# Eight more tile pairs of a four-layer trunk as products of half-size blocks, and one product placed earlier

## The chip, the cores and the metric

The kernel runs on one core of a Trainium2 chip. The metric is the device time of one execution in microseconds (us). The core's engines work side by side, each through its own queue in order: TensorE (PE) multiplies, VectorE (DVE) and GpSimd (POOL) add and subtract, ScalarE (ACT) copies and applies functions, SyncE (SP) starts most transfers.

## The reference, cut to what matters

Four layers, each `x += mixer(rmsnorm(x))` and then a layer end:

```
x += sigmoid(x @ pg_w[i]) * (p[i] @ pe_w[i])      # pg_w[i]: 1024 x 1024, pe_w[i]: 256 x 1024
```

Here x has 520 rows (512 of a prompt, 8 of a sample group) and 1024 columns. Everything is wanted in fp32. The mixers of the four layers are a matrix memory (layer 0), a gated short convolution (layer 1), windowed attention (layer 2) and causal pooling (layer 3); the code counts layers from 0.

## The kernel before

x lies in SBUF transposed, as eight tiles of 128 x 520 floats (`self.x[j]`). A product in fp32 is made from three products of numbers with shorter mantissas: an operand is split into a high part (`hi`, `wh`, made by ACT) and the rest (`lo`, `wl`, made by DVE from the operand and the high part), and PE adds up hi·wh, lo·wh and hi·wl. An output tile of 520 columns is made in two parts (256 and 264), so that a plain tile with eight tiles of input (`proj`) costs 8 x 3 x 2 = 48 matmuls.

`seven()` makes a pair of output tiles otherwise: weights and x are seen as 2 x 2 blocks (two output tiles by two halves of the input; two halves of x's 520 columns), and seven products of half size, of 12 matmuls of 260 columns each, with sums of weight blocks and sums of x blocks, take the place of eight: 84 matmuls for 96. The products are called "11", "T2", "T1", "21", "T3", "T4" and "22". The copy `s1` of "11" (line 378, ACT) must be made before "21" may add into the same accumulator; `u2` (line 381, DVE) and `u3` (line 390) are sums on the way to the outputs. "22" of a pair is held back in `self.pend` and issued later by `flush()`: in the middle of the next plain tile, or inside the next `seven()`. Before the change only the convolution's input projection in layer 1 is made so (19 pairs; `summed()`, lines 583 to 603, makes the row sums: four POOL subtractions, ACT copies `ha`, `hb`, DVE rests `la`, `lb` for each of four k).

The layer end is `embed()`. Each tile j takes 12 matmuls of the small product (`pe`) and 48 of the gate (`pg`), 60 in all. Then, in this chain: ACT's sigmoid (line 648), two DVE multiplies (line 650), a DVE add into x (line 651), ACT's `hi` of the next layer's input (line 470), ACT's square for the next norm (line 515 or 518), DVE's `lo` (line 471). The next tile's matmuls run meanwhile. Ahead of it `out_proj()` makes the x tiles one by one (line 628) and splits them.

Weights are brought in by SP (`wf`), split or summed ahead of use by ACT, DVE and POOL; a planner (`plan()`, `due()`) orders these operations by the cost of the matmuls that come before, and `pump()` issues them in the engines' queues between the other work. For some weights (`MOVED`) ACT makes the negative of `wh` and POOL starts a transfer that adds the weights to it in place of DVE's subtraction. Streams of small steps (`tick()`) are issued along the matmuls.

Of the kernel before, what the change touches and what calls it, by code (L numbers as in the profile page):

```python
# [22 lines left out]
KD = 8  # L23
# [16 lines left out]
NPLAIN = 3  # L40
HALF = T // 2
FBUFS, HBUFS, SBUFS = 4, 4, 4
MOVED = ("w_b", "w_bo")


class Item:


    def __init__(self, *keys, cost=5.76, life=None):
        self.keys, self.cost, self.life = keys, cost, life  # L50
        name, j = keys[0][:2]
        self.moved = name in MOVED and not (name == "w_b" and j % 16 == 0)


def paired(j):
# [4 lines left out]
def plan():  # L60

    out = []
    add = lambda *key, **kw: out.append(Item(key, **kw))

    def end(i, name, halves, begun=False):
        cs = range(2 if halves else 1)
        for c in cs:
            for j in range(2):
                if c or not begun:
                    last = c == len(cs) - 1 or i == 1  # L70
                    add(name, j, *([c] if halves else []), life=(2 - j) * 5.76 if last else None)
        for j in range(2, KD):
            for c in cs:
                add(name, j, *([c] if halves else []))
        for j in range(KD):
            if j % 4 == 0:
                add("w_pe", i, j // 4, cost=0, life=28.8)
            add("w_pg", i, j, cost=7.2)

    for hd in range(H):  # L80
        for j in (hd, 8 + hd, 16 + 2 * hd, 17 + 2 * hd, 32 + 2 * hd, 33 + 2 * hd):
            add("w_a", j)
    for j in range(16):
# [110 lines left out]
class Net:  # L194
# [47 lines left out]
    def make(self, i, op):  # L242

        if (i, op) in self.made:
            return
        self.made.add((i, op))
        nc, it = self.nc, self.items[i]
        t = self.wt.setdefault(i, {})
        f = lambda tile: tile.bitcast(F32)
        new = lambda tag, n=1024, pool=None, dt=F32R: (pool or self.wp).tile([P, n], dt, tag=tag, name=self.nm(tag))  # L250

        def high(k, tag, n=1024, pool=None):
            t["h" + k] = new(tag, n, pool)
            nc.scalar.activation(t["h" + k], t["w" + k], AF.Copy)  # L254

        def low(k, tag, n=1024, pool=None):
            t["l" + k] = new(tag, n, pool)
            if k == "1" and it.moved:
                nc.scalar.activation(t["l1"], f(t["h1"]), AF.Copy, scale=-1.0)  # L259
                key = it.keys[0]  # L260
                nc.gpsimd.dma_start(t["l1"], self.d[key[0]][key[1:]], accum_op=ALU.add)  # L261
                return
            nc.vector.tensor_sub(t["l" + k], t["w" + k], f(t["h" + k]))  # L263

        a, b = slice(0, 512), slice(512, 1024)
        sub = nc.gpsimd.tensor_sub
        if op in ("load", "load2"):
            n = 2 if op == "load2" else 1
            key = it.keys[n - 1]
            t[f"w{n}"] = self.wp.tile([P, 1024], F32, tag="wf", name=self.nm("wf"), bufs=FBUFS)  # L270
            nc.sync.dma_start(t[f"w{n}"], self.d[key[0]][key[1:]])
        elif op == "split":
            high("1", "wh")
            low("1", "wl")
        elif op == "sum":
            w1, w2 = t["w1"], t["w2"]
            s1, s2, s4 = (self.act()[:, :512] for _ in range(3))
            nc.gpsimd.tensor_add(s1, w2[:, a], w2[:, b])
            sub(s2, s1, w1[:, a])
            sub(w2[:, a], w1[:, a], w2[:, a])  # L280
            sub(s4, w1[:, b], s2)
            t.update(ws1=s1, ws2=s2, ws4=s4)
        else:
            k = op.removeprefix("high").removeprefix("low") or "1"
            step = high if op.startswith("high") else low
            if k[0] == "s":
                step(k, op[0] + "s", 512, self.sp)
            else:
                step(k, "w" + op[0])
# [49 lines left out]
            mm(out[j], wl, a[0][:, PARTS[j]], start=False, stop=stop)  # L339
        self.pump(0.72)  # L340

    def seven(self, keys, B, dst, done):

# [23 lines left out]
        def step():  # L367
            self.pump(1.44)
            self.tick()
# [12 lines left out]
        step()  # L382
        product(r5, part("s1"), "T1", True)
        step()
        product(r1, part("1", b), "21", False)
        nc.scalar.activation(dst[0][:, :HALF], r1, AF.Copy)
        step()
        self.flush()
        product(r6, part("2", a), "T3", False)
        add(u3, r6, s1)  # L390
        step()
        product(r4, part("2", b), "T4", True)
        pair = lambda x, n: x.rearrange("p (u c) -> p u c", u=2)[:, :, :n]
# [220 lines left out]
    def out_proj(self, name, y, i, begun=None):  # L614

        nc = self.nc
        xs = []
        first = begun or self.proj_pair(name, y, 8 if i == 2 else 16)
        self.pt = [self.act() for _ in range(2)]
        for k in range(2):  # L620
            nc.sync.dma_start(self.pt[k], self.d["pT"][i, k])
        for j in range(KD):
            if j in (3, 4):
                self.pt[j - 3] = self.split(self.pt[j - 3])
            if j == 0:
                *_, pair = first
            ps = pair[j] if j < 2 else self.proj(name, j, a=y)
            nc.vector.tensor_add(self.x[j], ps, self.x[j])  # L628
            xs.append(self.split(self.x[j]))
        self.look = 0  # L630
        return xs

    def embed(self, i, xs):

        nc, d = self.nc, self.d
        hs, we = [], None
        g0 = C_NG + (i + 1) * KD
        for j in range(KD):
            if j % 4 == 0:
                we = self.weights("w_pe", i, j // 4)  # L640
# [3 lines left out]
            if i == 3 and j == KD - 1:  # L644
                return self.final(xs, pe, hs)
            pg = self.proj("w_pg", i, j, a=xs)
            sg = self.act()
            nc.scalar.activation(sg, pg, AF.Sigmoid)  # L648
            for u in range(2):
                nc.vector.tensor_mul(sg[:, PARTS[u]], self.part(pe, u), sg[:, PARTS[u]])  # L650
            nc.vector.tensor_add(self.x[j], self.x[j], sg)
            if i < 3:
                hs.append(self.split(self.x[j], self.col(g0 + j)))
            else:
                hs.append(self.act())
                nc.scalar.activation(hs[j], self.x[j], AF.Copy, scale=self.col(C_FG + j))
            self.square_in(j)
        self.sums = {} if i == 0 else None
        self.finish_norm(hs, g0, 3, *((4, 1), (2, 3), (0, 0))[i], sums=self.sums)
        return hs  # L660

    def final(self, xs, pe, xg):
# [8 lines left out]
        xg.append(self.act())  # L671
# [46 lines left out]
    def mlstm(self, h, lay):  # L718
# [3 lines left out]
        with ExitStack() as st:  # L722
# [330 lines left out]
    def conv(self, h, lay):  # L1053
# [4 lines left out]
        with ExitStack() as st:  # L1058
# [387 lines left out]
    def pooling(self, h, lay):  # L1446
# [3 lines left out]
        with ExitStack() as st:  # L1450
# [68 lines left out]
    def run(self):  # L1519
# [32 lines left out]
        for i, (mixer, w) in enumerate(  # L1552
            ((self.mlstm, "w_ao"), (self.conv, "w_bo"), (self.attention, "w_co"), (self.pooling, "w_do"))
        ):
            with ExitStack() as lay:
# [4 lines left out]
            h = self.embed(i, xs)  # L1560


OUTS = {
# [124 lines left out]
```

## Time and profile before

| | |
|---|---|
| median of three executions | 2163.52 us (2162.26 to 2165.96) |
| the profiled execution | 2164.99 us |
| its span | 2163.2 us |
| PE busy | 2131.4 us, 99% |
| DVE, ACT, POOL busy | 1388.3, 899.8, 406.6 us |
| TensorE's granted clock, mean | 0.999 |

The span runs from the first to the last instruction in the trace; the 1.8 us beside it belong to the execution and not to the engines' work. Busy time of PE counts a matmul from its start to a modelled end, so idle time between matmuls and the list of waits say more than the 99%.

### The profile page before, as it was taken

How to read it: one execution, taken by the hardware profiler on the slowest of the kernel's cores; microseconds unless marked ns; L12 is line 12 of the kernel's file. 1: busy time of each engine (PE TensorE's matmuls, PEld its weight loads, DVE VectorE, ACT ScalarE, POOL GpSimd, SP SyncE). 2: the span in 40 equal slices, each digit the busy share in tenths (PEclk: the TensorE clock that was granted, in tenths of full speed). 3: DMA queues.
4: the chain of work that ended last, by engine and by line, in shares of the span. 5: the costliest groups of instructions: out<-in, count | busy, mean ns of one | idle time of the engine just before them, and what ended most of it. 6: DMA issues, size and time to landing. Idle time of an engine off the chain costs nothing.

```text
span 2163.2 us, 42666 instructions
## 1 busy us (share of the span) xinstructions
PE 2131.4 (99%) x17560; PEld 2111.3 (98%) x17560; DVE 1388.3 (64%) x3064; ACT 899.8 (42%) x1434; POOL 406.6 (19%) x487
## 2 busy tenths in 40 slices
PE   8999999999999999999999999999999999999998
PEld 8999999999999999999999999999999999999998
DVE  7677667653566666651478887787876566676434
ACT  6445443432455554564333333333344342222233
POOL 1111100100035545521014332332320000000000
PEclk9999999999999999999999999999999999999999
DMA  5654454332266676678333465555555233222421
GB/s 164 195 174 140 160 179 160 99 98 92 85 147 158 158 177 154 157 191 190 91 130 118 159 200 179 180 171 177 184 162 178 95 110 98 89 97 92 126 79 50
DMA packets 112951, 305.22 MB, mean 141 GB/s; under 512 B 34260, under 2 KB 38612, under 8 KB 110708
## 3 DMA queue, kind: packets, MB, share of 16 engines
q1 hardware_dynamic: 104404, 272.54, 38.9%
q0 software_dynamic: 8208, 29.89, 8.0%
q8 instruction: 138, 2.26, 0.4%
q14 instruction: 57, 0.47, 0.1%
q10 hardware_dynamic: 144, 0.06, 0.0%
HBM read 279.63 MB, written 22.82 MB: 140 GB/s over the span
## 4 chain that ended last, share of the span: by engine, by line
PE 76%; DVE 9%; DMA 5%; issue 4%; ACT 4%; POOL 2%; SPq 0%; ACTq 0%; DVEq 0%; POOLq 0%
PE ps L335 21%; PE ps L339 20%; PE ps L337 20%; DVE wl L263 2%; ACT wh L254 1%; PE ax L337 1%; PE ax L339 1%; PE ax L335 1%; PE ax L363 1%; PE ax L365 1%; PE ax L1335 1%; PE ax L364 1%; DMA kc<-kc 1%; DVE kc L460 1%; DMA wl<-w_b 1%
## 5 line engine op out<-in xcount | busy, mean ns | idle before, releaser
L335 PE MATMUL ps<-hi,wh 128*128 128x256 f32 x4672 | 963.5, 288 | 2.5 <-DVE a L486 1.5
L339 PE MATMUL ps<-hi,wl 128*128 128x256 f32 x4672 | 940.4, 283 | 0.9 <-DMA wl<-w_bo 0.7
L337 PE MATMUL ps<-lo,wh 128*128 128x256 f32 x4672 | 938.7, 282 | 0.4 <-DVE lo L1137 0.2
L335 PEld LDWEIGHTS ps<-hi,wh 128*128 128x128 f32 x4672 | 726.0, 188 | 8.6 <-issue 1.5
L337 PEld LDWEIGHTS ps<-lo,wh 128*128 128x128 f32 x4672 | 724.8, 188 | 0.8 <-DVE lo L1137 0.4
L339 PEld LDWEIGHTS ps<-hi,wl 128*128 128x128 f32 x4672 | 723.0, 188 | 1.5 <-DMA wl<-w_bo 0.9
L263 DVE TENSOR_TENSOR wl<-wf,wh 128x1024 fp32r<-128x1024 f32 x287 | 363.4, 1270 | 159.4 <-ACT wh L254 156.8
L254 ACT ACTIVATE wh<-wf 128x1024 fp32r<-128x1024 f32 x344 | 360.9, 1053 | 158.2 <-issue 90.9
L1212 POOL TENSOR_TENSOR a<-a,a 32x520 f32<-32x520 f32 x48 | 70.3, 1465 | 282.6 <-ACT a L503 103.1
L503 ACT ACTIVATE a<-ps 128x520 f32<-128x520 f32 x42 | 47.5, 1130 | 137.4 <-PE ps L339 118.9
L628 DVE TENSOR_TENSOR x<-ps,x 128x520 f32<-128x520 f32 x32 | 22.3, 698 | 122.8 <-PE ps L339 122.7
L1213 POOL TENSOR_TENSOR a<-a,a 32x520 f32<-32x520 f32 x48 | 70.8, 1475 | 129.9 <-DVE a L1211 117.1
L490 ACT ACTIVATE a<-a 128x520 f32<-128x520 f32 x42 | 26.8, 639 | 155.2 <-DVE a L486 155.2
L467 ACT ACTIVATE hi<-x 128x520 fp32r<-128x520 f32 x32 | 20.4, 639 | 156.4 <-DVE x L628 156.4
L486 DVE TENSOR_TENSOR a<-ps,a 128x520 f32<-128x520 f32 x85 | 58.9, 692 | 21.0 <-PE ps L339 17.6
L263 DVE TENSOR_TENSOR ls<-a,hs 128x512 fp32r<-128x512 f32 x57 | 64.5, 1142 | 12.0 <-ACT hs L254 12.0
L650 DVE TENSOR_TENSOR a<-ax,a 128x256 f32<-128x256 f32 (+1 forms) x62 | 23.7, 423 | 72.6 <-ACT a L648 72.6
L1238 ACT ACTIVATE S<-S,nmx 128x128 f32<-128x128 f32 (+1 forms) x96 | 39.9, 417 | 66.7 <-DVE nmx L1235 66.5
L460 DVE CUSTOM_DVE_ANT_0 kc<-kc,qb 128x128 f32<-128x128 f32 (+1 forms) x192 | 54.4, 340 | 14.2 <-DMA kc<-kc 14.2
L460 DVE CUSTOM_DVE_ANT_0 vc<-vc,pb 128x128 f32<-128x128 f32 (+1 forms) x192 | 62.9, 384 | 0.0
L261 POOL DMA_DIRECT2D wl<-w_b x41 | 36.3, 885 | 137.8 <-ACT wl L259 122.2
L259 ACT ACTIVATE wl<-wh 128x1024 fp32r<-128x1024 f32 x57 | 60.5, 1061 | 1.8
(344 smaller groups left out, 2874.8 us busy)
## 6 DMA issues: line engine op xcount, KB each, us to landing
wf<-w_c SPq DMA_DIRECT2D x80, 512.0 KB
wf<-w_a SPq DMA_DIRECT2D x64, 512.0 KB
wf<-w_b SPq DMA_DIRECT2D x64, 512.0 KB
wl<-w_b POOLq DMA_DIRECT2D x41, 512.0 KB, 6.6
wf<-w_pg SPq DMA_DIRECT2D x32, 512.0 KB
wf<-w_d SPq DMA_DIRECT2D x32, 512.0 KB
pb<-scr_p SPq DMA_DIRECT2D x8, 1292.0 KB
Ci<-C_in SPq DMA_DIRECT2D x16, 512.0 KB
```

The costliest lines, as they stand in the source:

```text
L254: nc.scalar.activation(t["h" + k], t["w" + k], AF.Copy)
L259: nc.scalar.activation(t["l1"], f(t["h1"]), AF.Copy, scale=-1.0)
L263: nc.vector.tensor_sub(t["l" + k], t["w" + k], f(t["h" + k]))
L335: mm(out[j], wh, a[0][:, PARTS[j]], start=start, stop=False)
L337: mm(out[j], wh, a[1][:, PARTS[j]], start=False, stop=False)
L339: mm(out[j], wl, a[0][:, PARTS[j]], start=False, stop=stop)
L460: self.nc.vector.tensor_tensor_reduce(junk, a, b, 1.0, 0.0, ALU.mult, ALU.add, out)
L486: nc.vector.tensor_mul(dst[:, :T], ps, self.r)
L503: nc.scalar.activation(dst, split(ps), AF.Copy)
L1212: nc.gpsimd.tensor_mul(b[:32], t[:32], cs[0])
L1213: nc.gpsimd.tensor_mul(a[:32], a[:32], cs[1])
L1238: nc.scalar.activation(blk, blk, AF.Exp, bias=nmx[:, i : i + 1], scale=SCALE, accum_out=l[:, i : i + 1])
```

## The change

In each layer's end the gate's tiles (1, 2) and (4, 5) are made by `seven()`: 84 matmuls for a pair in place of 96. The row sums of x that this needs are made by the new `crossed()`, one step for each pair of x tiles (k, k + 4): four POOL subtractions of 128 x 260, two ACT copies and two DVE subtractions of 128 x 520. It is queued as a stream when tile k + 4 of `out_proj` is done, and what is left of it is issued (`drain`) ahead of the first pair. `beside()` gives buffers for it. Inside `seven()` the held product "22" of the pair before now comes behind "T1" rather than behind "21"; this holds for the convolution too. Tile j + 1 of a pair is ended (`early`) behind "T4", and tile j behind "22", which is issued in the middle of the next tile's gate. The weights of these pairs are summed by POOL (four operations), and the low part of a pair's first weight goes by the POOL transfer (`moved`).

```diff
+EPAIRS = (1, 4)
...
-            add("w_pg", i, j, cost=7.2)
+            if j in EPAIRS:
+                out.append(Item(("w_pg", i, j), ("w_pg", i, j + 1), cost=12.96))
+            elif j - 1 not in EPAIRS:
+                add("w_pg", i, j, cost=7.2)
...
         product(r5, part("s1"), "T1", True)
         step()
+        self.flush()
         product(r1, part("1", b), "21", False)
         nc.scalar.activation(dst[0][:, :HALF], r1, AF.Copy)
         step()
-        self.flush()
         product(r6, part("2", a), "T3", False)
         add(u3, r6, s1)
         step()
         product(r4, part("2", b), "T4", True)
         pair = lambda x, n: x.rearrange("p (u c) -> p u c", u=2)[:, :, :n]
         add(pair(dst[1], HALF), pair(v, HALF), u3.unsqueeze(1).broadcast_to([P, 2, HALF]))
+        if early:
+            early()
         step()
         self.pend = last
...
             xs.append(self.split(self.x[j]))
+            if j > 3:
+                self.side.gens.append(self.crossed(j - 4, xs))
...
+    def crossed(self, k, xs):
+
+        nc, B = self.nc, self.xsums
+        a, b = slice(0, HALF), slice(HALF, T)
+        sub = nc.gpsimd.tensor_sub
+        t, u = self.x[k], self.x[k + 4]
+        ta, tb = self.act(), self.act()
+        sub(ta[:, a], t[:, b], t[:, a])
+        sub(ta[:, b], u[:, b], ta[:, a])
+        sub(tb[:, a], u[:, b], t[:, b])
+        sub(tb[:, b], u[:, a], ta[:, b])
+        for _ in range(4):
+            yield
...
+        hs = room("ha"), room("hb")
+        for h, x in zip(hs, (ta, tb)):
+            nc.scalar.activation(h, x, AF.Copy)
+        yield
+        ls = room("la"), room("lb")
+        for h, l, x in zip(hs, ls, (ta, tb)):
+            nc.vector.tensor_sub(l, x, h.bitcast(F32))
...
+        def two(j, we):
+            sg = self.act(), self.act()
+            end = lambda n: lambda: ends(j + n, part(we, j + n), sg[n], sg[n])
+            self.seven((("w_pg", i, j), ("w_pg", i, j + 1)), self.xsums, sg, end(0), end(1))
+
+        for j in range(KD):
+            if j % 4 == 0:
+                we = self.weights("w_pe", i, j // 4)
+            if j in EPAIRS:
+                self.side.drain()
+                two(j, we)
+            elif j - 1 not in EPAIRS:
+                pe = part(we, j)
+                if i == 3 and j == KD - 1:
+                    return self.final(xs, pe, hs)
+                pg = self.proj("w_pg", i, j, a=xs)
+                ends(j, pe, self.act(), pg)
```

The order of instructions shows where this puts the work. First ACT's queue at the start of layer 0's end, before; `x_85` to `x_92` are the eight x tiles, and a name's number tells one buffer use from another:

```order
L648 ACT_TABLE_LOAD
L648 ACTIVATE a_6525<-ps_6474 128x520
L470 ACTIVATE hi_6530<-x_85,cols 128x520
L515 ACTIVATE a_6534<-x_85 128x520
L254 ACTIVATE wh_6551<-wf_6316 128x1024
L648 ACTIVATE a_6605<-ps_6550 128x520
```

The same place after (the sigmoid is line 696 now, `hi` 479, the square 524, a weight's high part 261, the row sums' copies 666, `s1` 385):

```order
L696 ACT_TABLE_LOAD
L696 ACTIVATE a_6596<-ps_6523 128x520
L479 ACTIVATE hi_6601<-x_85,cols 128x520
L524 ACTIVATE a_6605<-x_85 128x520
L666 ACTIVATE ha_6607<-a_6542 128x520
L666 ACTIVATE hb_6608<-a_6543 128x520
L261 ACTIVATE wh_6619<-wf_6350 128x1024
L385 ACTIVATE a_6626<-ax_6623 128x260
L394 ACTIVATE a_6615<-ax_6623 128x260
```

The copies `ha`, `hb` of the fourth row sum (k = 3) stand behind the whole end of tile 0, and `s1` of the first pair behind them. Then the second pair of the same layer, ACT's queue after the change; `x_86` is tile 1, `x_88` tile 3, and `hs` the high part of a weight sum:

```order
L696 ACTIVATE a_6615<-a_6615 128x520
L479 ACTIVATE hi_6830<-x_86,cols 128x520
L527 ACTIVATE a_6834<-x_86 128x520
L261 ACTIVATE hs_6837<-a_6721 128x512
L696 ACTIVATE a_6865<-ps_6764 128x520
L479 ACTIVATE hi_6870<-x_88,cols 128x520
L527 ACTIVATE a_6874<-x_88 128x520
L261 ACTIVATE wh_6877<-wf_6594 128x1024
L385 ACTIVATE a_6886<-ax_6883 128x260
```

The end of tile 1 now comes directly ahead of the end of tile 3, and the second pair's `s1` (the last row) behind both. In layer 2 two of the four row sums come late; ACT's queue there after the change:

```order
L696 ACTIVATE a_20780<-ps_20707 128x520
L479 ACTIVATE hi_20785<-x_85,cols 128x520
L524 ACTIVATE a_20789<-x_85 128x520
L666 ACTIVATE ha_20791<-a_20726 128x520
L666 ACTIVATE hb_20792<-a_20727 128x520
L666 ACTIVATE ha_20805<-a_20799 128x520
L666 ACTIVATE hb_20806<-a_20800 128x520
L261 ACTIVATE wh_20817<-wf_20520 128x1024
L385 ACTIVATE a_20824<-ax_20821 128x260
```

Four copies stand there in place of two, those of k = 2 and of k = 3. Next POOL's queue in layer 0 after the change, around the fourth row sum (lines 653 to 656); lines 285 to 288 sum the second pair's weights:

```order
L268 DMA wl_6457<-w_pg 128x1024
L653 TENSOR_TENSOR a_6542<-x_88 128x260
L654 TENSOR_TENSOR a_6542<-x_92,a_6542 128x260
L655 TENSOR_TENSOR a_6543<-x_92,x_88 128x260
L656 TENSOR_TENSOR a_6543<-x_92,a_6542 128x260
L285 TENSOR_TENSOR a_6719<-wf_6594 128x512
L286 TENSOR_TENSOR a_6720<-a_6719,wf_6562 128x512
L287 TENSOR_TENSOR wf_6594<-wf_6562,wf_6594 128x512
L288 TENSOR_TENSOR a_6721<-wf_6562,a_6720 128x512
```

The sums for the second pair follow at once, as soon as their weights have landed. Last the convolution: PE's queue in the last of three pairs in a row, before, where "T1" (`ps_8507`) ends and "21" (`ax_8505`) begins:

```order
L363 MATMUL ps_8507<-ha_7740,hs_8432 128x260
L364 MATMUL ps_8507<-la_7742,hs_8432 128x260
L365 MATMUL ps_8507<-ha_7740,ls_8461 128x260
L363 MATMUL ax_8505<-hi_7289,wh_8333 128x260
L364 MATMUL ax_8505<-lo_7305,wh_8333 128x260
L365 MATMUL ax_8505<-hi_7289,wl_8337 128x260
```

And after, at the end of the same "T1" (`ps_8605`):

```order
L370 MATMUL ps_8605<-ha_7838,hs_8539 128x260
L371 MATMUL ps_8605<-la_7840,hs_8539 128x260
L372 MATMUL ps_8605<-ha_7838,ls_8559 128x260
L370 MATMUL ps_8466<-hi_7387,hs_8458 128x260
L371 MATMUL ps_8466<-lo_7403,hs_8458 128x260
L372 MATMUL ps_8466<-hi_7387,ls_8462 128x260
```

The twelve matmuls of the pair before's "22" (`ps_8466`) now stand between "T1" and "21".

## Rows read from the trace of the kernel before

**Rows 1.** The page's head: span, and busy time of each engine.

```profile
span 2163.2 us, 42666 instructions
...
PE 2131.4 (99%) x17560; PEld 2111.3 (98%) x17560; DVE 1388.3 (64%) x3064; ACT 899.8 (42%) x1434; POOL 406.6 (19%) x487
```

**Rows 2.** Waits of PE: what waited, for what; us in total, times, longest.

```profile
PE ps L335 <- ACT a L1542: 5.2, 1, 5.2
PE ax L363 <- ACT a L378: 5.0, 6, 0.8
PE ax L1306 <- DVE S L1298: 4.2, 4, 2.0
```

**Rows 3.** Line 378 (`s1`): who waited for it, us and times.

```profile
  PEld ax L363: 6.3, 6
```

**Rows 4.** Timeline of ACT, layer 0's end: start, duration, line, idle before.

```profile
553.82 0.60 ACT L648 ACTIVATE a<-ps 128x520 f32<-128x520 f32 x1 [3.57 <-PE ps L339]
555.99 0.73 ACT L470 ACTIVATE hi<-x,cols 128x520 fp32r<-128x520 f32 x1 [1.56 <-DVE x L651]
556.63 0.62 ACT L515 ACTIVATE a<-x 128x520 f32<-128x520 f32 x1
557.16 1.04 ACT L254 ACTIVATE wh<-wf 128x1024 fp32r<-128x1024 f32 x1
561.00 0.60 ACT L648 ACTIVATE a<-ps 128x520 f32<-128x520 f32 x1 [2.80 <-PE ps L339]
```

**Rows 5.** Timeline of PE where the second tile's matmuls begin.

```profile
553.62 0.40 PE L335 MATMUL ax<-hi,wh 128*128 128x256 f32 x2
```

**Rows 6.** Timeline of ACT, layer 2's end.

```profile
1715.36 0.60 ACT L648 ACTIVATE a<-ps 128x520 f32<-128x520 f32 x1 [3.55 <-PE ps L339]
...
1718.70 1.04 ACT L254 ACTIVATE wh<-wf 128x1024 fp32r<-128x1024 f32 x1
```

**Rows 7.** Timeline of PE, the convolution's third pair: "T1", "21", "22".

```profile
719.47 0.28 PE L365 MATMUL ps<-ha,ls 128*128 128x260 f32 x1
720.59 0.39 PE L363 MATMUL ax<-hi,wh 128*128 128x260 f32 x1 [0.83 <-ACT a L378]
...
722.12 0.28 PE L363 MATMUL ps<-hi,hs 128*128 128x260 f32 x1
```

**Rows 8.** Timelines of ACT and DVE at the same place.

```profile
720.16 0.37 ACT L378 ACTIVATE a<-ax 128x260 f32<-128x260 f32 x1
...
718.67 0.70 DVE L394 TENSOR_TENSOR a<-ps,a 128x520 f32<-128x520 f32 x1
```

**Rows 9.** Timelines of ACT and DVE: a row sum's copies and rests.

```profile
659.32 0.62 ACT L600 ACTIVATE ha<-a 128x520 fp32r<-128x520 f32 x1
...
659.98 0.70 DVE L603 TENSOR_TENSOR la<-a,ha 128x520 fp32r<-128x520 f32 x1 [3.27 <-ACT ha L600]
```

**Rows 10.** Timeline of DVE in layer 0's end.

```profile
554.46 0.76 DVE L650 TENSOR_TENSOR a<-ax,a 128x256 f32<-128x256 f32 x2 [4.25 <-ACT a L648]
556.76 0.76 DVE L471 SCALAR_TENSOR_TENSOR lo<-x,cols,hi 128x520 fp32r<-128x520 f32 x1 [0.80 <-ACT hi L470]
```

**Rows 11.** Timelines of DVE and POOL in the convolution.

```profile
704.42 0.67 DVE L263 TENSOR_TENSOR ls<-a,hs 128x512 fp32r<-128x512 f32 x1
...
706.02 2.61 DVE L263 TENSOR_TENSOR ls<-a,hs 128x512 fp32r<-128x512 f32 x1
...
706.49 1.58 POOL L278 TENSOR_TENSOR a<-wf 128x512 f32<-128x512 f32 x1
```

**Rows 12.** Timeline of PE, the first matmuls of the program.

```profile
8.86 0.64 PE L335 MATMUL ps<-hi,a 128*64 128x256 f32 x2
9.29 0.64 PE L337 MATMUL ps<-lo,a 128*64 128x256 f32 x2
...
14.08 0.40 PE L335 MATMUL ps<-hi,a 128*64 128x256 f32 x2
14.32 0.40 PE L337 MATMUL ps<-lo,a 128*64 128x256 f32 x2
```

More of the change, by code (lines that the diff above doesn't have):

```diff
@@ L51, in __init__ @@
         name, j = keys[0][:2]
-        self.moved = name in MOVED and not (name == "w_b" and j % 16 == 0)
+        self.moved = name in MOVED and not (name == "w_b" and j % 16 == 0) or name == "w_pg" and len(keys) > 1
 def paired(j):
@@ L249, in make, with new @@
         f = lambda tile: tile.bitcast(F32)
-        new = lambda tag, n=1024, pool=None, dt=F32R: (pool or self.wp).tile([P, n], dt, tag=tag, name=self.nm(tag))
+        def new(tag, n=1024, pool=None):
+            if pool is self.ap:
+                return self.act(F32R, tag)[:, :n]
+            return (pool or self.wp).tile([P, n], F32R, tag=tag, name=self.nm(tag))
         def high(k, tag, n=1024, pool=None):
@@ L340, in mm6, with seven @@
         self.pump(0.72)
-    def seven(self, keys, B, dst, done):
+    def seven(self, keys, B, dst, done, early=None):
         nc = self.nc
@@ L618, in out_proj @@
         first = begun or self.proj_pair(name, y, 8 if i == 2 else 16)
+        self.side, self.xsums = Stream(1), {n: [] for n in ("11", "21", "22", "T1", "T2", "T3", "T4")}
+        self.streams = [*self.streams, self.side]
         self.pt = [self.act() for _ in range(2)]
@@ L629, in out_proj, with room, beside, part @@
             xs.append(self.split(self.x[j]))
+            if j > 3:
+                self.side.gens.append(self.crossed(j - 4, xs))
         self.look = 0
         return xs
+    def crossed(self, k, xs):
[10 more added lines that the diff above has]
+            yield
+        def room(s):
+            self.spare -= 1
+            return self.act(F32R, s, self.ep if self.spare >= 0 else None)
+        hs = room("ha"), room("hb")
[5 more added lines that the diff above has]
+            nc.vector.tensor_sub(l, x, h.bitcast(F32))
+        for n, (h, l), c in (("11", xs[k], a), ("21", xs[k + 4], a), ("22", xs[k + 4], b),
+                             ("T1", (hs[0], ls[0]), a), ("T2", (hs[0], ls[0]), b),
+                             ("T3", (hs[1], ls[1]), a), ("T4", (hs[1], ls[1]), b)):
+            B[n].append((h[:, c], l[:, c]))
+        yield
+    def beside(self, lay, n):
+        pool = lambda name, **kw: lay.enter_context(self.tc.tile_pool(name=self.nm(name), **kw))
+        self.sp = pool("ws", bufs=SBUFS)
+        self.ep, self.spare = pool("ep", bufs=n), n
     def embed(self, i, xs):
         nc, d = self.nc, self.d
-        hs, we = [], None
+        hs, we = [None] * KD, None
         g0 = C_NG + (i + 1) * KD
-        for j in range(KD):
-            if j % 4 == 0:
-                we = self.weights("w_pe", i, j // 4)
+        def part(we, j):
             pe = self.aux(), self.aux()
@@ L643, in embed, with ends @@
                 self.mm6(pe, we, ((j % 4) * 2 + k) * P, self.pt[k], k == 0, k == 1)
[L644 to L647, printed above, removed]
+            return pe
+        def ends(j, pe, sg, pg):
             nc.scalar.activation(sg, pg, AF.Sigmoid)
@@ L652, in embed @@
             if i < 3:
[L653 removed]
+                hs[j] = self.split(self.x[j], self.col(g0 + j))
             else:
[L655 removed]
+                hs[j] = self.act()
                 nc.scalar.activation(hs[j], self.x[j], AF.Copy, scale=self.col(C_FG + j))
             self.square_in(j)
+        def two(j, we):
[14 more added lines that the diff above has]
+                ends(j, pe, self.act(), pg)
         self.sums = {} if i == 0 else None
@@ L670, in final @@
         x, sg, sq = self.x[j], self.act(), self.act()
-        xg.append(self.act())
+        xg[j] = self.act()
         ch = lambda t, c: t[:, c * n : (c + 1) * n]
@@ L778, in mlstm @@
         ex = lay.enter_context(tc.tile_pool(name="mly", bufs=16))
+        self.beside(lay, 3)
         self.streams = [self.gate]
@@ L1149, in conv @@
             nc.sync.dma_start(d["o_conv_s"], so)
+        self.beside(lay, 3)
         return y
@@ L1205, in attention @@
         self.finish = finish
+        self.sp, self.ep, self.spare = self.ap, None, 0
         return y
@@ L1475, in pooling @@
             nc.sync.dma_start(d["o_pool_s"], sp[:, :, 1:16])
+        self.beside(lay, 10)
         return y, first
@@ L1559, in run @@
                 xs = self.out_proj(w, y, i, first)
-            h = self.embed(i, xs)
+                h = self.embed(i, xs)
 OUTS = {
```

## The prediction

> **What bounds the kernel now.** I read the page's head first: PE is busy 99% of a span of 2163.2 us [rows 1]. So the question is not which engine is full but how much PE waits, and the waits of PE come next. The longest stands at the program's start (5.2 us), the next belongs to the very routine that the change uses: "21" of a pair waits for ACT's copy `s1`, 5.0 us in 6 times [rows 2], and the weight load ahead of it waits 6.3 us in the same 6 times [rows 3]. Nothing in the four layer ends is near the head of that list. So matmuls that are taken away there are worth their full time, and every new wait of PE costs its full time.
>
> The timeline of a layer end shows the pace: tile 0's sigmoid starts at 553.82, tile 1's at 561.00 [rows 4], 7.18 us for 60 matmuls, 0.1197 us each. PE runs ahead without a break: the next tile's first matmul begins at 553.62, 0.20 us before that sigmoid [rows 5]. I count all times below from S, tile 0's sigmoid. ACT's chain is `hi` at S+2.17, square at S+2.81, and what follows begins at S+3.34 [rows 4]. Layer 2 has the same steps: 1715.36 and, for what follows the square, 1718.70 [rows 6]. This chain has no influence on PE before the change, because nobody in the layer end waits for what ACT does there.
>
> **What is taken away.** Eight pairs lose one product of 12 matmuls: 12 x 0.1197 = 1.436 us each, **11.5 us** in all.
>
> **The product placed earlier.** In the convolution's third pair in a row "T1" has its last matmul at 719.47, "21" would start 0.12 later, and starts at 720.59 after a wait of 0.83; its first matmul lasts 0.39 and "22" follows at 722.12 [rows 7]. The copy that it waits for begins at 720.16 [rows 8], behind two weight operations of 1.05 on ACT. With 12 matmuls of "22" between, "21" wants to start at 721.03, by which time the copy is done. "22" itself then needs its accumulator free, which the DVE sum begun at 718.67 and lasting 0.70 [rows 8] has given back at 719.37, 0.2 before. So I take the whole 6 waits, **5.0 us**, as gained; the bounds are 0 (another wait, like that DVE sum, ends last) and 6.3 [rows 3].
>
> **New waits at the first pair, layers 0, 1 and 3.** The pair's "11" starts at S-0.20 and needs only x. "T2" starts at S+1.24 and wants the fourth row sum at its tenth matmul, S+2.3: `ha` first, then `la` one matmul later (S+2.43). By the order, ACT makes `ha` behind tile 0's sigmoid, `hi` and square, so from S+3.34, 0.62 long; `la` on DVE starts 0.66 after `ha` does and takes 0.70 [rows 9], so it is ready at S+4.70. The wait is 4.70-2.43 = **2.3 us**, and nothing covers it: PE has no other work in its queue. POOL can make it longer. The order puts the second pair's four weight sums there at about this time, and where a sum (1.58) runs beside DVE, a DVE subtraction of 0.67 took 2.61 [rows 11], 1.9 more. Ahead of `la` stands one such operation, `lo` of tile 0 at S+2.94 [rows 10, 4]. Held twice the wait is 6.2, held not at all 2.3; I take half of one hold, 0.9, since the sums have to meet just these 2 us: 3.2 each, **9.6** in three layers (6.9 to 18.5).
>
> The Trainium skill (SBUF — State Buffer, "Who interferes with whom") says that a DVE instruction with two inputs in SBUF contends with a GpSimd instruction that reads SBUF, and that the later of the two blocks until the first has finished. The trace agrees (0.67 to 2.61). By that rule alone both `lo` and `la` would be held whenever a sum is running, and this wait would be nearer its upper end.
>
> **At the second pair, same layers.** "21" starts 36 matmuls after "11". Were tile 3's sigmoid on time, 0.20 after "11" starts, "21" would be wanted at S3+4.11 (S3 is that sigmoid), and `s1` would come behind `hi`, square (next at S3+3.34) and a weight (1.04), 0.37 long: S3+4.75, a wait of 0.65. But the order puts the end of tile 1 directly ahead: its small product ends 24 matmuls before "11", so its multiplies start about S3-3.1, its `hi` 1.53 later (554.46 to 555.99, [rows 10, 4]), and square and a weight sum fill ACT to about S3+0.2, while DVE still has tile 1's `lo`, a norm's sum and a weight's rest to do before tile 3's multiplies. That moves the chain by 0.75 to 1.3. I take a wait of 1.6 each, **4.8** (2.0 to 6.0).
>
> **Layer 2.** The copies of two row sums stand behind tile 0 there. The fourth `ha` is the third copy, so it begins two steps of 0.53 later, and `la` behind it on DVE ends about S+6.1: a wait of 3.65 (to 4.4 with a hold). At the second pair tile 3's sigmoid gets a buffer that "T2" of that pair still reads; it starts when "T1" starts, and `s1` comes 3.34+1.04+0.37 = 4.75 later, where "T1" lasts 1.44: a wait of 3.3, up to 5.0 with a late weight transfer. I take 4.2. Together **7.9** (6.95 to 9.4).
>
> **Left at nothing.** The 80 ACT copies and 80 DVE operations more are hidden by idle time (42% and 64% busy [rows 1]) except where named; without that cover a pair of copies would cost 1.1. POOL's subtractions of the other row sums run under `out_proj`'s matmuls.
>
> **Sum.** New waits 9.6+4.8+7.9 = 22.3; gains 11.5+5.0 = 16.5; **+5.8 us**. The profiled execution is 2164.99, its span 2163.2; it lies 1.5 above the median of the three runs, and what I forecast is a median, so 2163.5+5.8 = **2169.3 us**.
>
> **Rivals.**
> *The waits stay fewer (faster).* A wait of PE lets ACT and DVE catch up. If the wait at "T2" is the only one in each layer, 2.3 each, because it gives the later `s1` the time that they lack, the new waits are 9.2 and the time 2163.5+9.2-16.5 = 2156.2. For it speaks that ACT is idle 3.57 and 2.80 us ahead of the sigmoids [rows 4]; against it that a chain behind its own sigmoid moves with PE, so a delay ahead of it gives it nothing. It decides from new waits under 12.2 us, 3 for each layer.
> *Gain and waits cancel (no change).* With the lower bounds, 6.9+2.0+6.95 = 15.9, less 16.5: 2162.9; up to 2167.8 all of it is the same case.
> *POOL holds DVE (slower still).* Two holds at each first pair and the upper bounds elsewhere: 18.5+6.0+9.4 = 33.9, less 16.5: 2180.9, or 2185.9 if the convolution gives nothing back.
> *The clock falls.* At the program's start, after 5 us of rest, two matmuls took 0.43 us from start to start (8.86 to 9.29), later 0.24 (14.08 to 14.32) [rows 12]: the lower and the higher level, 1.2 and 2.4 GHz. The rows lie 5.2 us apart. If one wait of over 3 us in each layer end brought the lower level back for such a stretch, PE would lose half of it, 2.6, each time: 10 more, 2179.7. Against it: waits of up to 2.0 inside the program [rows 2] left the mean clock high, and none here is as long as that first rest.
> The Trainium skill (TensorE: Matmul & The Clock Gate, "Why this matters for your kernels") warns that gaps of PE between bursts bring the half clock back; no longer gap inside this program shows it.
>
> **How the numbers follow.** Forecast (waits over 20.8 us but no second hold everywhere): 0.42. No change: 0.27. Fewer waits: 0.20. POOL holds DVE: 0.07. Clock: 0.04. A measurement of this kernel tells 0.2%, 4.3 us, from no change: faster is under 2159.2, slower over 2167.8. The forecast lies only 1.5 above that line; its own range is 2167.8 to 2176. Slower 0.53, same 0.27, faster 0.20. The range for 8 in 10 takes in the middle of the faster case and of POOL's holds: 2155 to 2181.
>
> **What would show it.** PE's waits would list "T2" on `la` (line 670) or `ha` (666) four times, over 2 us each, 3.6 or more in layer 2; "21" on `s1` (385) in the second pairs, 4 times; and no wait of "21" in the convolution. From one layer end's first sigmoid to its last, 2 x 1.44 less and 4 to 8 more. It would be wrong if the copies of the last row sum came before tile 0's `hi`, if waits at "T2" were under 1, or if the earlier "22" got a wait of its own in the convolution.

## The result, and the profile after

The changed kernel takes 2181.78 us (median of five, 2175.08 to 2183.78), the kernel before 2163.52 (five, 2162.26 to 2167.07). The ratio is 1.0072, 95% interval 1.005 to 1.0094: **slower by some 16 us** (11 to 20). The ratio is that of the means, 2180.0 and 2164.4; the medians lie 18.3 apart. Forecast was 2169.3, slower, with a range of 2155 to 2181. The median lies 0.8 above the range, the ratio puts the time at 2179.1, inside it; the direction is right, the forecast difference is a third of the measured one. The profiled execution is 2181.78 us itself.

The page's head of the changed kernel, against [rows 1]:

```profile
span 2180.0 us, 42848 instructions
PE 2132.8 (98%) x17464; PEld 2109.6 (97%) x17464; DVE 1458.3 (67%) x3144; ACT 943.1 (43%) x1514; POOL 529.9 (24%) x591
```

96 matmuls are gone and PE is as long busy as before. That is the first hint. The list of cores has span and mean granted clock, 0.999 before:

```profile
core 0: 2180.0 us, clock 0.992
```

The waits of PE in the changed kernel (for what; us in total, times, longest), by line, to be read beside [rows 2]:

```profile
PE ax L372 <- DMA wl<-w_pg: 5.5, 5, 2.0
PE ax L370 <- ACT ha L666: 5.2, 3, 2.1
PE ps L342 <- ACT a L1612: 5.0, 1, 5.0
...
PE ax L370 <- ACT a L385: 3.6, 2, 3.4
PE ax L371 <- DVE la L670: 3.2, 4, 1.2
PE ps L346 <- DMA wl<-w_b: 2.2, 2, 1.8
PE ax L370 <- DVE a L388: 1.9, 1, 1.9
```

The convolution's six waits on `s1` are gone from the list; five new kinds stand in the layer ends, 19.4 us together, and waits on the convolution's weight transfer (2.2). Each wait holds the weight load ahead of the matmul a little longer, so the weight loads' list of the same five kinds sums to 22.9:

```profile
PEld ax L372 <- DMA wl<-w_pg: 6.5, 5, 2.2
PEld ax L370 <- ACT ha L666: 5.8, 3, 2.3
...
PEld ax L370 <- ACT a L385: 4.3, 3, 3.6
PEld ax L371 <- DVE la L670: 4.0, 4, 1.4
...
PEld ax L370 <- DVE a L388: 2.3, 2, 2.1
```

What follows such a wait is seen in a table of short stretches. Each row has a stretch and its length, then for PE, PEld, DVE, ACT and POOL the busy time with the number of instructions in brackets; the third number from the end is the granted clock. These rows are layer 1's first pair, around and behind its two waits:

```profile
1059.00:1060.00 1.00, 0.00 (x1) 0.01 (x1) 0.84 (x2) 1.00 (x3) 0.92 (x2) 1.00 0.00 0
1060.00:1061.00 1.00, 0.39 (x1) 0.18 (x1) 1.00 (x1) 1.00 (x2) 1.00 (x2) 0.97 0.00 0
1061.00:1062.00 1.00, 0.44 (x2) 0.44 (x3) 1.00 (x2) 0.69 (x2) 1.00 (x1) 0.50 0.00 0
1062.00:1064.00 2.00, 2.00 (x11) 2.00 (x11) 2.00 (x2) 0.00 (x0) 2.00 (x2) 0.50 0.05 8
1064.00:1066.00 2.00, 2.00 (x11) 2.00 (x11) 2.00 (x3) 0.00 (x0) 0.34 (x1) 0.50 0.00 0
1066.00:1068.00 2.00, 2.00 (x12) 2.00 (x11) 0.37 (x2) 0.34 (x2) 0.00 (x0) 0.56 0.42 86
1068.00:1070.00 2.00, 2.00 (x19) 2.00 (x18) 0.81 (x2) 0.99 (x2) 0.00 (x0) 1.00 0.44 176
```

PE is "busy" all the time from 1062 on, but makes 11 matmuls in 2 us where it makes 19 afterwards: it runs at the lower of its two levels, 1.2 GHz. Seven microseconds of it cost 3.4. The other falls in the layer ends, one in layer 0, two in layer 2 and one in layer 3:

```profile
559.00:561.00 2.00, 2.00 (x13) 2.00 (x12) 2.00 (x2) 0.00 (x0) 2.00 (x2) 0.55 0.04 8
561.00:563.00 2.00, 2.00 (x12) 2.00 (x12) 2.00 (x3) 0.00 (x0) 0.17 (x1) 0.60 0.00 0
...
1726.00:1728.00 2.00, 2.00 (x14) 2.00 (x13) 2.00 (x3) 0.47 (x2) 1.66 (x1) 0.64 0.00 0
1728.00:1730.00 2.00, 2.00 (x11) 2.00 (x11) 1.40 (x2) 0.00 (x0) 1.95 (x1) 0.51 0.01 4
1753.00:1755.00 2.00, 1.33 (x7) 1.33 (x8) 1.90 (x4) 1.56 (x3) 0.00 (x0) 0.71 0.00 0
1755.00:1757.00 2.00, 2.00 (x11) 2.00 (x11) 1.07 (x1) 0.46 (x2) 0.00 (x0) 0.50 0.66 174
...
2112.00:2114.00 2.00, 2.00 (x13) 2.00 (x12) 0.92 (x1) 2.00 (x4) 1.31 (x1) 0.56 0.04 10
2114.00:2116.00 2.00, 2.00 (x12) 2.00 (x12) 2.00 (x2) 0.80 (x2) 1.99 (x2) 0.58 0.01 4
```

Summed in the same way (one minus the clock, times the stretch), layer 0's end loses 1.7, layer 1's 3.4, layer 2's 3.4 in two places and layer 3's 1.7: 10.2 us. Elsewhere there is one fall in the convolution (1.7) and one in the attention (1.7). So the layer ends come out by rows: -11.5 (products) + 22.9 (waits) + 10.2 (clock) = +21.6. The sigmoids' times say the same by another way. From a layer's first sigmoid to its last (in layer 3 to tile 6's):

| stretch | before | after | difference |
|---|---|---|---|
| start to layer 0's first sigmoid | 553.82 | 552.80 | -1.02 |
| layer ends 0, 1, 2, 3 | 50.22, 50.32, 50.26, 43.04 | 54.27, 54.84, 58.97, 47.33 | +4.05, +4.52, +8.71, +4.29 |
| to layer 1's end (the convolution) | 452.58 | 448.92 | -3.66 |
| to layer 2's end, to layer 3's end, and the tail | 608.42, 330.88, 23.66 | 608.68, 330.61, 23.58 | -0.09 |
| span | 2163.2 | 2180.0 | +16.8 |

The layer ends are 21.57 longer, as the sum says. The waits of the first pairs in layers 0 to 2 stand where the order had put them. ACT, PE, DVE and POOL in layer 0's first pair (start, duration, line):

```profile
555.61 0.62 ACT L524 ACTIVATE a<-x 128x520 f32<-128x520 f32 x1
556.13 0.62 ACT L666 ACTIVATE ha<-a 128x520 fp32r<-128x520 f32 x1
...
556.81 0.38 PE L370 MATMUL ax<-ha,hs 128*128 128x260 f32 x1 [1.52 <-ACT ha L666]
558.38 0.39 PE L371 MATMUL ax<-la,hs 128*128 128x260 f32 x1 [1.18 <-DVE la L670]
...
556.79 1.53 DVE L670 TENSOR_TENSOR la<-a,ha 128x520 fp32r<-128x520 f32 x1 [0.16 <-ACT ha L666]
...
556.15 1.62 POOL L286 TENSOR_TENSOR a<-a,wf 128x512 f32<-128x512 f32 x1
```

`ha` comes 3.33 after the sigmoid (552.80), behind the square; `la` takes 1.53 in place of 0.70 [rows 9] beside POOL's sum. "T2" waits 2.70 in two pieces.

### The profile page after: what moved, and what is told of

It is laid out like the page before. It is cut to its first block, busy times and chain, and to the rows that moved or that the text cites. A ratio compares the mean times of both kernels' runs of the same rounds, so it can differ in the third digit from the quotient of the medians.

```text
span 2180.0 us, 42848 instructions
## 1 busy us (share of the span) xinstructions
PE 2132.8 (98%) x17464; PEld 2109.6 (97%) x17464; DVE 1458.3 (67%) x3144; ACT 943.1 (43%) x1514; POOL 529.9 (24%) x591
## 4 chain that ended last, share of the span: by engine, by line
PE 74%; DVE 10%; DMA 6%; issue 4%; ACT 4%; POOL 2%; SPq 0%; POOLq 0%; ACTq 0%; DVEq 0%
PE ps L342 19%; PE ps L346 19%; PE ps L344 19%; PE ax L370 2%; PE ax L372 2%; DVE wl L270 2%; PE ax L371 2%; DMA wl<-w_b 1%; PE ps L370 1%; PE ps L371 1%; PE ps L372 1%; DVE vc L469 1%; ACT wh L261 1%; PE ax L1404 1%; DMA kc<-kc 1%
## 5 line engine op out<-in xcount | busy, mean ns | idle before, releaser
L342 PE MATMUL ps<-hi,wh 128*128 128x256 f32 x4416 | 912.1, 288 | 2.6 <-DVE a L510 0.9
L346 PE MATMUL ps<-hi,wl 128*128 128x256 f32 x4416 | 888.1, 282 | 2.9 <-DMA wl<-w_b 2.2
L344 PE MATMUL ps<-lo,wh 128*128 128x256 f32 x4416 | 888.1, 282 | 0.4 <-DVE lo L1204 0.2
L342 PEld LDWEIGHTS ps<-hi,wh 128*128 128x128 f32 x4416 | 686.2, 189 | 9.1 <-issue 2.1
L346 PEld LDWEIGHTS ps<-hi,wl 128*128 128x128 f32 x4416 | 684.0, 188 | 3.7 <-DMA wl<-w_b 3.0
L344 PEld LDWEIGHTS ps<-lo,wh 128*128 128x128 f32 x4416 | 685.4, 189 | 0.8 <-DVE lo L1204 0.4
L270 DVE TENSOR_TENSOR ls<-a,hs 128x512 fp32r<-128x512 f32 x81 | 89.6, 1113 | 22.2 <-ACT hs L261 17.2
L639 DVE TENSOR_TENSOR x<-ps,x 128x520 f32<-128x520 f32 x32 | 22.3, 697 | 90.9 <-PE ps L346 90.8
L372 PE MATMUL ax<-hi,wl 128*128 128x260 f32 x216 | 63.2, 293 | 5.5 <-DMA wl<-w_pg 5.5
L370 PE MATMUL ax<-hi,wh 128*128 128x260 f32 x216 | 63.2, 293 | 3.6 <-ACT a L385 3.6
L371 PE MATMUL ax<-lo,wh 128*128 128x260 f32 x216 | 63.0, 292 | 0.0
```

Source lines behind the costliest of these rows:

```text
L342: mm(out[j], wh, a[0][:, PARTS[j]], start=start, stop=False)
L344: mm(out[j], wh, a[1][:, PARTS[j]], start=False, stop=False)
L370: mm(out, w[0][:, c], hi, start=start and k == 0, stop=False, **go)
L371: mm(out, w[0][:, c], lo, start=False, stop=False, **go)
L372: mm(out, w[1][:, c], hi, start=False, stop=k == 3, **go)
```

## The experiments

All times are medians. Kernels of one group ran on the same chip and share the runs of the kernel before there: 2165.4 (e1 to e4), 2165.7 (e5, e6, e8, e9), 2165.9 (e10 to e12), 2167.6 (e13). Differences in us are taken from the ratios.

**The product placed earlier, alone** (e1), in the kernel before:

```diff
         product(r5, part("s1"), "T1", True)
         step()
+        self.flush()
         product(r1, part("1", b), "21", False)
...
-        self.flush()
```

> The kernel before with only the held product "22" placed behind "T1". Theory A (a wait moved, and TensorE's clock reacts to it): the six waits of 0.83 us at "21" go (5.0), but waits on the added transfer of weights come in the convolution (2.2 us in the changed kernel's profile) and one fall of the clock (about 1.7): 1 to 3 us faster, 2160.5 to 2162.5. Theory B (my prediction's step: nothing comes late next): 5.0 faster, 2158.5.

2157.8, ratio 0.9963 (0.9951 to 0.9974): 8 us faster, 5.6 to 10.6. In the profile the convolution's stretch is 446.79 long, 5.8 under the one before, and has no fall of the clock; the waits on `s1` are off the list, two on the weight transfer (1.7) are on it:

```profile
PE ax L1306 <- DVE S L1298: 4.8, 4, 2.0
PE ps L339 <- DMA wl<-w_b: 1.7, 2, 0.9
```

Theory B is nearer: this part of the change is worth what the prediction gave it (5.0), or somewhat more. Of the 8.2 between the two profiles' spans 5.8 stand in the convolution; what makes the rest, where this edit moves no product, is open. Theory A took the fall of one profile for a rule.

**The pairs alone** (e2): the changed kernel with "22" back behind "21".

```diff
-        self.flush()
         product(r1, part("1", b), "21", False)
         nc.scalar.activation(dst[0][:, :HALF], r1, AF.Copy)
         step()
+        self.flush()
```

> The changed kernel with "22" put back behind "21": the pairs in the layer ends alone. Theory A (waits of 19 us at the layer ends, falls of the clock of about 12 us there, 11.5 us saved): about 19 us slower than before, 2182 to 2184. Theory B (prediction: waits of 22.3, no falls): 10.8 slower, 2174. The six waits at "21" in the convolution must be back in either.

2186.4, ratio 1.0098 (1.0084 to 1.0113): 21 us slower, as theory A has it. The mean clock is 0.992 again, the waits on `s1` are back (8.8 us in 9 times, the convolution's six with 5.0 among them). The pairs cost 21, the moved product gives 8 back, and the whole change is slower by 16: the parts add up within their intervals.

**A wait by itself** (e3, e4): no pair, nothing saved, only three waits. In layers 0 to 2 one more matmul at the head of tile 1's gate reads a tile that is not ready:

```diff
+            if late is not None:
+                self.nc.tensor.matmul(self.part(ps, 0), late[:, :P], late[:, PARTS[0]], start=True, stop=True)
...
-            pg = self.proj("w_pg", i, j, a=xs)
+            pg = self.proj("w_pg", i, j, a=xs, late=hs[0][0] if j == 1 and i < 3 else None)
```

e4 has `hs[0][1]` (lo) for `hs[0][0]` (hi).

> The kernel before, without any pair: in layers 0 to 2 one more matmul ahead of tile 1's gate reads tile 0's hi, which ACT has ready at about S+2.9, so that PE waits some 1.7 us three times; its product is overwritten. Theory B (a wait costs its length): 5.1 us and 0.4 for the matmuls, 2169. Theory A (the clock falls behind waits): up to 1.7 to 3.4 us more for each wait behind which the granted clock falls; in the changed kernel a single wait of 1.46 had no fall and one of 1.84 had, so this length is at the edge: 2169 to 2175.

> The same with tile 0's lo in place of hi, ready at about S+3.7: PE waits some 2.5 us three times. Theory B: 7.5 and 0.4, 2171.5. Theory A: a fall behind each wait, granted clock 0.5 for some 3.4 or 6.8 us, 1.7 or 3.4 us lost each time: 2176.5 to 2181.5, and the profile shows the granted clock under 1 right behind each of the three waits.

e3: 2171.1, ratio 1.0027 (1.0017 to 1.0037), +5.7; three waits of 1.56, 1.54 and 1.56 us and the added matmuls explain it, and the clock stays at 1.00 behind all three:

```profile
557.00:559.00 2.00, 2.00 (x19) 2.00 (x19) 1.19 (x1) 0.00 (x0) 0.00 (x0) 1.00 0.03 8
...
1062.00:1064.00 2.00, 2.00 (x20) 2.00 (x19) 0.87 (x1) 0.00 (x0) 0.00 (x0) 1.00 0.10 18
...
1724.00:1726.00 2.00, 2.00 (x19) 2.00 (x19) 0.97 (x1) 0.00 (x0) 0.00 (x0) 1.00 0.04 10
```

e4: 2176.1, ratio 1.0049 (1.0036 to 1.0062), +10.7 (single times from 2171.7 to 2180.9, wider than the kernel before). Its three waits are 2.44, 2.43 and 2.44 long. Short stretches behind each of the three, columns as above:

```profile
555.00:557.00 2.00, 1.40 (x7) 1.43 (x8) 1.28 (x2) 1.14 (x2) 0.00 (x0) 0.71 0.04 8
557.00:559.00 2.00, 2.00 (x11) 2.00 (x10) 0.40 (x1) 0.00 (x0) 0.00 (x0) 0.50 0.36 39
...
1063.00:1065.00 2.00, 2.00 (x19) 2.00 (x18) 0.80 (x1) 0.00 (x0) 0.00 (x0) 1.00 0.14 18
...
1723.00:1725.00 2.00, 1.56 (x7) 1.59 (x8) 1.29 (x2) 0.98 (x2) 0.00 (x0) 0.55 0.00 0
1725.00:1727.00 2.00, 2.00 (x13) 2.00 (x12) 0.23 (x1) 0.00 (x0) 0.00 (x0) 0.60 0.35 100
```

Behind the first and the third the clock falls for some 3.4 us (1.7 lost each), behind the second, of the same length, it does not. So a wait of this kernel can cost 1.7 more than its length, and whether it does is not decided by the length alone. The changed kernel's spread, 2175 to 2184, goes with its clock: the two short executions (2175.1, 2176.1) have a mean of 0.995 and 0.994, the three long ones (2181.8 to 2183.8) of 0.992 or 0.993. The spread of e4 does not: its executions of 2173.5 and 2180.9 have 0.997 both, so part of its +10.7 is not settled.

**The copies first** (e5): the row sum's rest ahead of tile 0's sigmoid.

```diff
                 pg = self.proj("w_pg", i, j, a=xs)
+                if j == 0 and i != 2:
+                    self.side.drain()
                 ends(j, pe, self.act(), pg)
```

> The changed kernel with the rest of the fourth row sum (ha, hb, la, lb) issued ahead of tile 0's sigmoid in layers 0, 1 and 3; layer 2 as it was. Theory A (ACT's order makes T2 wait, and the clock falls behind those waits): the waits on ha and la in layers 0 and 1 (2.7 us each) go, and with them falls of 1.7 and 3.4 us; layer 3's wait on u2 (1.9) goes too, its wait on the weight transfer (2.0) stays: 10 to 13 us faster than the changed kernel, 2169 to 2172. Theory B (POOL's sums hold DVE, so that la is late wherever ACT makes ha): some 1.2 us of wait stays in each, 2175 to 2178.

2175.9, ratio 1.0044 (1.003 to 1.0058), 9.5 over the kernel before, where the change is 16 over it: 6 of A's 10 to 13, between the two theories. The waits at "T2" in layers 0 and 1 are gone (ACT's order made them), but a wait of 1.75 on `u2` takes their place in each, and the second pair's transfer is later (2.21 in layer 0, 1.60 in layer 2):

```profile
PE ax L372 <- DMA wl<-w_pg: 6.9, 5, 2.2
...
PE ax L370 <- DVE a L388: 3.5, 2, 1.8
PE ax L370 <- ACT ha L666: 2.1, 1, 2.1
```

**The low part by DVE** (e6):

```diff
-        self.moved = ... or name == "w_pg" and len(keys) > 1
+        self.moved = ...
```

> The changed kernel with the pairs' first low part made by DVE's subtraction in place of ACT's negative and POOL's transfer. Theory A (the transfer of some 6 to 8 us is late, DVE has room): the five waits on the transfer (5.5 us) go, and the fall behind the one of 2.0 us in layer 3 (1.7): about 2174 to 2176. Theory B (DVE's 1.2 us more for each pair make la, u2 late): the waits move to la and u2, 2179 to 2184.

2178.8, ratio 1.0057 (1.0044 to 1.0071). The transfer's waits go from the list, and the waits move on, as theory B says, but not to the places that it named: to `ha` (7.9 us in 4, layer 3's first pair now among them) and `s1` (6.5 in 4), while `la` has 3.5 and `u2` 1.0. One of these waits, 3.37 us at layer 2's second pair, is the longest in any layer end so far, and no fall follows it:

```profile
1750.82 0.39 PE L370 MATMUL ax<-hi,wh 128*128 128x260 f32 x1 [3.37 <-ACT a L385]
...
1752.00:1754.00 2.00, 2.00 (x19) 2.00 (x18) 1.22 (x3) 1.34 (x2) 0.00 (x0) 1.00 0.45 145
```

With 3.4 us less lost to the clock in its profile it comes out some 3 us under the changed kernel by the ratios, which the intervals don't separate.

**Both, and without layer 2's second pair** (e8, e9): e5's edit in all layers, e6's edit, `Stream(2 if i == 2 else 1)` for the row sums; e9 makes tiles 4 and 5 of layer 2 plainly.

> Both edits together, and the row sums' steps issued twice as fast in layer 2. Theory A: what is left is tile 3's sigmoid in layer 2, which waits for its buffer (3.4 us at "21", and a fall of 1.7); from the time before go 11.5 us of products and 3.7 to 5.8 us in the convolution: 2151 to 2156. Theory B (pairs in the layer ends cost more in other engines' time than they save): not under e1_flush_only, 2158 or more.

> The same with layer 2's second pair made plainly, so that its late sigmoid holds nobody. Theory A: 1.44 us of products come back, the wait of 3.4 and the fall of 1.7 go: 3 to 4 us under e8_first_and_dve, 2148 to 2153. Theory B: no difference, or 1.4 slower.

e8: 2178.3, ratio 1.0052 (1.004 to 1.0064). e9: 2171.7, ratio 1.0027 (1.0018 to 1.0035). Theory A failed on e8 by over 20 us. The waits at "T2" (but for 0.7 in layer 2) and on the pairs' transfers are gone and stand at "21" instead:

```profile
PE ax L370 <- ACT a L385: 14.7, 8, 4.3
...
PE ax L370 <- DVE a L388: 4.4, 3, 1.9
```

Theory A had not seen that the edit makes waits of its own: in layers 2 and 3 the row sums' copies, now ahead of tile 0's sigmoid, come late themselves, and behind them the sigmoid starts 3.4 and 3.1 us later than before, counted from the first pair's first matmul. `s1` stands behind the sigmoid, and "21" waits 2.98 and 4.33 for it. Layer 2's second pair alone is worth 5 us to leave out (the ratios' difference, 0.0025), where 3 to 4 were expected from its 3.36 us wait with a fall behind it.

**The second pairs alone** (e10, e11): only tiles (4, 5) of layers 0, 1 and 3, low part by DVE. In e11 the end of the tile ahead is cut in two, and its `hi`, `lo` and square are issued behind the pair's `s1`:

```diff
         nc.scalar.activation(s1, r1, AF.Copy)
+        if first:
+            first()
...
+            if hold:
+                later.append(lambda: rest(j))
```

> Of the changed kernel only the pairs (4, 5) of layers 0, 1 and 3, with the low part made by DVE, and "22" behind "T1". Theory A (a pair pays 1.44 us less the waits that its profile shows; these have one wait of 1.1 us on s1 each, too short for the clock to fall): nothing won or lost against e1_flush_only, 2157 to 2159. Theory B (pairs in a layer end cost something that the waits of PE don't show): 2161 or more.

> The same with tile 3's hi, lo and square issued behind the pair's s1 in place of ahead of it. Theory A (ACT's order makes the wait on s1): the three waits go, 4 us under e10_second_pairs, 2153 to 2155. Theory B (the wait moves on to u2 on DVE, which has the same work to do): as e10_second_pairs within 1.5.

e10: 2163.7, ratio 0.999 (0.9982 to 0.9999), 6 over e1 and not even with it: three waits on `s1` (4.4 us) and three more on `u2` (2.3) eat more than the 4.3 of products. With the weight loads they come to 7.9 (5.0 and 2.9), and the layer ends are 4.0 longer than in e1's profile: theory A's rule holds, and its waits were too short. e11: 2158.6, ratio 0.9969 (0.9959 to 0.9979), 4.5 under e10, as theory A had it: the waits on `s1` are gone by order alone, 2.4 on `u2` stay. Against e1 these three pairs win nothing that the intervals show.

**All pairs of e9 with `s1` first** (e12), and **six pairs with "T4" ahead of "T3"** (e13; pairs (1, 2), (4, 5) in layers 0 and 1, (1, 2) in layer 2, (4, 5) in layer 3):

```diff
+        product(r4, part("2", b), "T4", True)
+        step()
         product(r6, part("2", a), "T3", False)
         add(u3, r6, s1)
-        step()
-        product(r4, part("2", b), "T4", True)
```

> e9_seven_pairs with hi, lo and square of the tile ahead of every pair issued behind that pair's s1. Theory A (order on ACT): the seven waits on s1 (11.5 us) and the falls in layers 2 and 3 (1.7 and 3.4 us) go, the waits on u2 stay: 2154 to 2159. Theory B (DVE, held by POOL's sums, is what the first pairs wait for): the waits move to u2, 2164 to 2170.

> e12_all_s1_first without layer 3's first pair (six pairs left), and "T4" ahead of "T3" in every pair, so that u2 has 1.44 us more. Theory A (the order of products and copies makes the waits): layer 3's waits of 3.8 and 0.7 us and the fall behind them go, and the three waits of 1.3 on u2 as well: 8.6 us of products are saved against e1_flush_only with under 2 us of waits left, 2149 to 2155. Theory B (DVE's work is the bound in the first pairs): u2 is late all the same, 2157 to 2162.

e12: 2163.4, ratio 0.9994 (0.9985 to 1.0003), 7 under e9: the waits on `s1` fall from 11.5 to 0.7 us, those on `u2` rise from 3.5 to 7.8 (four first pairs, 3.8 in layer 3). The time lies between the two theories: the order is one cause, and DVE's work, by where the waits moved, the other; no run takes POOL's sums away to show how much of it is their hold. e13: 2155.2, ratio 0.9947 (0.9933 to 0.996), the fastest here. Its list no longer has a wait on `s1` or `u2`:

```profile
PE ax L1387 <- DVE S L1379: 5.6, 4, 2.0
...
PE ps L346 <- DMA wl<-w_b: 1.7, 3, 1.2
...
PE ax L371 <- DVE la L672: 0.7, 1, 0.7
```

It beats both kernels. Against e1 (0.9963) it is 3.5 us faster, where theory A counted on 8.6 less some 2 of waits, and the intervals overlap, so that six pairs are worth more than none is likely and not shown. In its profile the layer ends 0 to 3 last 47.67, 47.68, 46.85 and 41.71 from sigmoid to sigmoid, shorter than before by 9.9 in all, but the stretch from layer 1's end to layer 2's first sigmoid is 616.56, longer by 8.1. In both, 3.4 is a moved mark and no time of PE: layer 2's first sigmoid stands behind the row sums' copies and starts 3.63 us after the first pair's first matmul, where before it started 0.20 behind the next tile's first matmul, as in layer 0 [rows 4, 5]:

```profile
1707.05 0.28 PE L370 MATMUL ax<-hi,wh 128*128 128x260 f32 x1
...
1710.68 0.61 ACT L700 ACTIVATE a<-ps 128x520 f32<-128x520 f32 x1
```

By PE's matmuls the layer ends are 6.5 shorter, and layer 2's own, with one pair, is as long as before (50.28 and 50.26). The stretch ahead of it is 4.7 longer: 1.7 is a fall of the clock in the attention, behind a wait of 1.99, 1.4 are longer waits there (5.6 against [rows 2]'s 4.2), 0.8 is a wait on DVE ahead of it, and 0.8 is not settled.

## Why the prediction was right or wrong, point by point

**The bound: right.** Waits of PE decide, and there was no room in the layer ends: +21.6 by rows, and e3 and e4 show that a wait there costs its full length. That it can cost more is the step that failed, below.

**Products taken away, 11.5: right.** No run has this saving without the waits; the sum -11.5+22.9+10.2 meets the 21.57 of the sigmoids' times.

**Product placed earlier, 5.0: right in kind, somewhat small.** e1's profile has 5.8 in that stretch; the changed kernel kept 3.7, because a weight transfer was 1.84 late there and the clock fell behind it. "Another wait ends last" was named as the lower bound; it took 2.1 of 5.8 in the one profile.

**First pairs: right place, right size.** 2.70 in layers 0 and 1 for a term of 3.2, in the order `ha`, `la` as worked out, `la` held once by POOL (1.53 for 0.70). In layer 2 2.97 for 3.65. In layer 3 the place was wrong: "11" waited first, 2.02 on the weight transfer, which gave `ha` its time, and then "T3" 1.88 on `u2`: 3.90 for 3.2. The transfer was not in my sum there.

**Second pairs: wrong place, fair size in layer 2.** Layers 0, 1 and 3 don't wait on `s1` in the changed kernel but at "11" on the transfer, 1.46, 0.84 and 0.39, 2.7 for 4.8; the delay at "11" gave ACT the time. Once the transfer was taken away (e6), `s1` did wait, 1.10, 1.12 and 0.88. In layer 2 3.35 on `s1` and 0.78 on the transfer, 4.13 for 4.2.

**The sum of waits, 22.3: right in size, and partly by luck:** 19.4 at the matmuls, 22.9 with the weight loads. The transfer in layers 0, 1 and 3 (4.7) and layer 3's `u2` (1.9) were not in it and took the place of what did not come, `s1` in three second pairs (4.8) and "T2" in layer 3 (3.2). Of the signs named, "T2" waited in three layers of four, "21" on `s1` in one second pair of four, and the convolution's waits went.

**The step that failed: the clock.** The sum had nothing for it; it was a rival with a chance of 0.04, put down because waits of 2.0 inside the program had left the clock high and no new wait would be as long as the rest at the start. The runs show that shorter waits are enough. In the layer ends 10.2 us went to the clock: 5.1 behind the first pairs of layers 0 and 1, where two waits of 1.5 and 1.2 follow each other, and 5.1 behind waits of 2.10, 3.35 and 2.02. That this meets the rival's price of 10 is luck: its condition, a wait of over 3 us in each layer end, held in layer 2 alone. My reason against it was no reason: the trace before had no wait between 2.0 and 5 at which to see it. The sentence of the Trainium skill (TensorE: Matmul & The Clock Gate, "Why this matters for your kernels"), that gaps of PE bring the half clock back, stood against the row that I preferred. e4 agrees with it in kind, with two falls behind three waits of 2.4; the third, and e6's wait of 3.37, have none, and there the measurement decides.

**POOL's hold on DVE: real, and no more than the half hold that the sum had in the first pairs.** Later subtractions are held again (1.77 and 2.29 for layer 3's two ahead of `u2`), and so are the two ahead of `u2` in e5 (1.76 and 2.30): the first of each such two took 0.67 by itself [rows 11]. That this makes `u2` the next wait in e5 and e12 is read from these rows; no run is without POOL's sums. In [rows 11] the held instruction begins 0.47 before POOL's sum, so that row shows a hold, but not that the later one has to wait. `la` in layer 0 shows this: it begins at 556.79, inside POOL's sum (556.15 to 557.77), and ends 0.55 behind it.

**The faster rival: refuted.** A wait does give later chains time, as layers 0, 1 and 3 show at the second pair, but a wait elsewhere took its place: new waits were 19, not under 12.2.

## What to carry to other kernels

Where PE is the bound, a saved product is worth its time only if every operand of the shorter form is early in its engine's queue: count where each copy stands in the order, and expect that a wait taken away uncovers the next one in the same chain (`ha`, then `u2`, then `s1`). Price a wait of PE of some 2 us, or two shorter ones close together, with a fall of the clock behind it as well as its length, as a likely cost and not a sure one; that no row shows a fall at that length says nothing where no row has a wait of that length. And time the harmless-looking part of a change alone: here one moved line was the gain, and the eight pairs in their first order lost more than twice as much.

## What the runs showed of the hardware that I had not expected

TensorE's granted clock went to 0.50 behind single waits of 1.84 (the convolution), 2.02, 2.11, 2.4 (two of three in e4) and 3.35 us, stayed there for some 3.4 us or, in layer 1's end, twice that, and came back by itself while PE worked on; each such stretch cost 1.7 or 3.4 us. It also fell behind, or during the second of, two waits close together, of 1.5 and 1.2. Behind three single waits of 1.5 (e3) it stayed at 1.00, and behind one of 2.43 (e4) and one of 3.37 (e6) too. The same wait may so cost 1.7 us more or not from one execution to the next. The longest wait in the attention shows it best, for every kernel here has it: it is 1.94 to 2.11 us long in all fourteen profiles, nine have a fall within 2 us behind it (waits of 1.98 to 2.11) and five have none (1.94 to 2.02).
